# One more pair of feature tiles on the seven-product path of the second FFN, its operands made ready inside w_o

## The chip, the cores and the metric

The kernel runs on one core of a Trainium2 chip. The engines that matter here: TensorE (PE) multiplies matrices; VectorE (DVE), ScalarE (ACT) and GpSimd (POOL) do elementwise work; SyncE (SP) issues the DMAs that load weights. Each engine works through its own instructions in order and waits where an operand, or the memory for a result, isn't there yet. The metric is the device time of one execution in microseconds (us), the median of several runs.

## The reference, cut to what matters

One layer of a streaming encoder on 512 tokens of width 1024, all in float32: FFN 1, a mixer (recurrent branch and attention, merged, then `w_o`), FFN 2, each between two RMS norms. The change touches the end of the mixer and FFN 2:

```python
def swiglu(x, w1, w3, w2):
    return (jax.nn.silu(x @ w1) * (x @ w3)) @ w2

h = h + rms_norm(merged @ w_o[l], mix_post_g[l])
f = swiglu(rms_norm(h, ffn2_pre_g[l]), ffn2_w1[l], ffn2_w3[l], ffn2_w2[l])
h = h + 0.5 * rms_norm(f, ffn2_post_g[l])
```

`D_FF` is 2816, so w1 and w3 have 22 feature tiles of 128 columns each.

## The kernel before

**Split numbers.** TensorE multiplies in a rounded float32 format (fp32r). To keep float32 accuracy each operand is split into hi, a cast on ACT, and lo, the operand less hi, a subtract on DVE (`split2`, L191 and L192; the same two lines for plain weight tiles in `split_to`, L156 and L157). A product takes three matmuls: hi hi, lo hi, hi lo.

**Units and pair jobs.** A plain unit (`unit`, `mm_feat`, L201 to L203) makes one feature tile for all 512 tokens: 8 slices of k, three matmuls of 512 columns each, 24 in all. From some feature tile on, two tiles go together as pair jobs (class `Pairs`), one for w1 and one for w3: the product is seen as 2 x 2 blocks (two halves of k, two halves of the tokens, two feature tiles) and made by seven block products instead of eight (Strassen's scheme in Winograd's form). One block product (`mm_s`, L452 to L454) is 4 slices of k, three matmuls of 256 columns each, so a pair job has 84. The price is sums of blocks: S1 to S4 of each weight pair (L497 to L500, on POOL unless `eng` says otherwise), T1 to T4 of the activations (`sums`, L728 to L732), and all of them are split again. `Pairs.prep(m, i)` makes job m's weights ready in five steps: 0 the sums S12 and S34, 1 the split of the first raw tile, 2 of S12, 3 of S34, 4 of the half tile a22. While job n runs, `Pairs.run` issues steps 1 to 4 of job n + 1, step 0 of job n + 2 and the loads of job n + 3. `hooks` lets other work be issued inside a job. The order inside a job is a11, s1 (with T1), the last product of the job before (a22 with T4), s2 (with T2), a12, s4, s3 (with T3).

`NC1` = 6 and `NC2` = 4 say from which feature tile on FFN 1 and FFN 2 use pair jobs. In FFN 2 tiles 0 and 1 belong to the end of w_o's stage (below), tiles 2 and 3 are plain units (`swiglu_units`), tiles 4 to 21 are 18 pair jobs.

**w_o's stage** (`tok_gemm`). The first two of w_o's eight k slices are multiplied for all four token tiles first. Then, token tile by token tile, come the other six slices (L219 to L221); when a token tile t is whole, `norms` adds it to h and norms it for FFN 2: two Squares on ACT (L259), fg on DVE (L260, L261), some small steps, the new h (L264), Squares and products again (L275, L276), and the result hg (L282 on DVE for one half of the columns, L283 on ACT for the other). TensorE transposes hg (L292), `transpose_out` copies and splits it into uT (L301 ACT, L302 DVE), and `transpose_xf` copies it unsplit into xf (L309 ACT), from which the sums T are made. TensorE transposes tile t after the matmuls of tile t + 1. Instead of a fifth tile's matmuls come those of FFN 2's first four weight tiles (w1 and w3 of feature tiles 0 and 1, `first`) on the first 256 tokens: after the first of them the transposes of token tile 2, before the last those of tile 3. Then the same four weight tiles on the other 256 tokens, then `tok_gemm` ends.

**What sets the order.** The program's order is kept on each engine. `later(n, fn)` issues something n points further on; a point comes after every four k slices of a unit and after each block product. Weight tiles are loaded and split in the order of a list (`order`); splitting ahead stops at the first paired tile, whose raw tile `Pairs` takes instead.

**Slots.** All large tiles share 42 slots of SBUF (`NSLOT`), 4 KB per partition each. A tile takes a slot at its first write and gives it back after its last use. With none free, the instruction that writes first waits, and what is behind it on its engine.

**Ahead of the first pair job** of FFN 2, before: its steps 0 to 4, T1 to T4 and the splits of T1 to T3 are issued by `later` during the four plain units of tiles 2 and 3.

Of the kernel before, what the change touches and what calls it, by code (L numbers as in the profile page):

```python
# [13 lines left out]
ALU = mybir.AluOpType  # L14
# [37 lines left out]
def hybrid_layer(ctx: ExitStack, tc: tile.TileContext, a: dict, out: bass.AP):  # L52
# [91 lines left out]
    def dma_to(n):  # L144
        while st["dma"] < min(n, len(order)):
            dma_one(st["dma"])
            st["dma"] += 1
# [148 lines left out]
    def transpose_out(banks, t, xf=None):  # L296
        c = slice(t * P, (t + 1) * P)
        for half, ps in enumerate(banks):
            ks = slice(half * 4, half * 4 + 4)
            v = ps.rearrange("p (k c) -> p k c", k=4)  # L300
            act.activation(uT[:, 0, ks, c], v, AF.Copy)  # L301
            dve.tensor_tensor(out=uT[:, 1, ks, c], in0=v, in1=f32(uT[:, 0, ks, c]), op=ALU.subtract)  # L302
        if xf:
            transpose_xf(banks, t, xf)
# [4 lines left out]
            act.activation(xf[half, t // 2][:, :, (t % 2) * P : (t % 2 + 1) * P], v, AF.Copy)  # L309


    def tok_gemm(nm, xs, n, R, gpost_name, scale, gpre_name, first, x_to=None, xf=None, spill=False):

        F = n - R
        acc = {}
        w = {}

        def accs(t):  # L320
            if t not in acc:
                acc[t] = [bank("acc"), bank("acc")]
            return acc[t]

        pre = min(2, F)
        x_to = x_to or (lambda k: None)
        for k in range(pre):
            x_to(k + 1)
            w[k] = get(nm, k, ahead=pre - k + 1)
        if pre:  # L330
            for tt in ((0, 1), (2, 3)):
                for k in range(pre):
                    for t in tt:
                        mm_tok(accs(t), xs[k], t, w[k], k == 0, False)
                        if t % 2:
                            point()
        for k in range(pre, F):
            x_to(k + 2)
            w[k] = get(nm, k, ahead=2 + (R - 2) * (k + 1) // F)
            for t in range(NT):  # L340
                mm_tok(accs(t), xs[k], t, w[k], k == 0, False)
                if t % 2:
                    point()
        point(True)
        for k in range(F, n):
            x_to(k + 1)
            w[k] = get(nm, k, ahead=max(0, n - 1 - k), rawahead=2)
        gpost = bcast(gpost_name)
        gpre = bcast(gpre_name) if gpre_name else None
        us, trs = {}, {}  # L350
        split_to(st["get"] + len(first))
        dma_to(st["split"] + 2)
        for t in range(NT):
            for ns in ((0,), (1,)):
                for k in range(F, n):
                    mm_tok(accs(t), xs[k], t, w[k], k == 0, k == n - 1, ns)
            if not gpre_name:
                o = slot([P, D], name="o")

                def store(nn, c, t=t, o=o):  # L360
                    sp.dma_start(out=out[t * P : (t + 1) * P, c], in_=o[:, c])

                post_norm(acc[t], t, gpost, scale, o, store)
                continue
            if t == NT - 1:
                break
            if t >= 1:
                trs[t - 1] = transpose_mm(us[t - 1])
            if t == NT - 2:

                transpose_out(trs[t - 1], t - 1)
            us[t] = norms(acc[t], t, gpost, scale, gpre, spill)
            if t == NT - 2 and xf:
                transpose_xf(trs[t - 1], t - 1, xf)
            elif t == 1:
                transpose_out(trs[t - 1], t - 1, xf)
        if not gpre_name:
            return
        t = NT - 1
        ws, bs = [], []  # L380
        for i, key in enumerate(first):
            ws.append(get(*key, ahead=len(first) - 1 - i, rawahead=2))
            bs.append(bank("f"))
            if i == len(first) - 1:
                trs[t] = transpose_mm(us[t])
                transpose_out(trs[t], t)
                if xf:
                    transpose_xf(trs[t - 1], t - 1, xf)
                    transpose_xf(trs[t], t, xf)
            mm_feat(bs[i], ws[i], 0, 256)  # L390
            if i == 0:
                trs[t - 1] = transpose_mm(us[t - 1])
                us[t] = norms(acc[t], t, gpost, scale, gpre, spill)
                transpose_out(trs[t - 1], t - 1)
        get_ahead()
        for w_, b in zip(ws, bs):
            mm_feat(b, w_, 256, 512)
        return bs
# [58 lines left out]
    class Pairs:  # L457
# [13 lines left out]
        def prep(self, m, i, eng=None):  # L471
            if m >= len(self.jobs) or (m, i) in self.ready:
                return
            self.ready.add((m, i))
            k = self.k0 + 2 * m
            if i == 0:
                if k not in loaded or k + 1 not in loaded:
                    self.raws(m)
                s12, s34 = slot([P, 2 * QH], name="S12"), slot([P, 2 * QH], name="S34")
                self.w[m] = {"r": (raws.pop(k), raws.pop(k + 1)), "s": (s12, s34)}  # L480
            W = self.w[m]
            (ra, rb), (s12, s34) = W["r"], W["s"]
            a11, a12, a21, a22 = ra[:, :QH], ra[:, QH:], rb[:, :QH], rb[:, QH:]

            def both(src, w=2 * QH):
                hi = slot([P, w], F32R, name="whi")
                lo = slot([P, w], F32R, name="wlo")
                split2(hi, lo, src)
                return hi, lo

            def halves(p, a, b):
                W[a] = p[0][:, :QH], p[1][:, :QH]
                W[b] = p[0][:, QH:], p[1][:, QH:]

            if i == 0:
                e = eng or pool
                e.tensor_tensor(out=s12[:, :QH], in0=a21, in1=a22, op=ALU.add)  # L497
                e.tensor_tensor(out=s12[:, QH:], in0=s12[:, :QH], in1=a11, op=ALU.subtract)
                e.tensor_tensor(out=s34[:, QH:], in0=a12, in1=s12[:, QH:], op=ALU.subtract)
                e.tensor_tensor(out=s34[:, :QH], in0=a11, in1=a21, op=ALU.subtract)  # L500
            elif i == 1:
                halves(both(ra), "a11", "a12")
            elif i == 2:
                halves(both(s12), "s1", "s2")
            elif i == 3:
                halves(both(s34), "s3", "s4")
            elif i == 4:
                t = slot([P, 2, QH], F32R, name="w22")
                split2(t[:, 0, :], t[:, 1, :], a22)
                W["a22"] = t[:, 0, :], t[:, 1, :]  # L510
                del W["r"], W["s"]

        def run(self, tail, hooks={}):
# [208 lines left out]
    def pair_view(p):  # L722
        return lambda e, k: p[e][:, k, :]

    def sums(xf):

        t = [slot([P, 4, 256], name="T") for _ in range(4)]
        pool.tensor_tensor(out=t[2], in0=xf[1, 1], in1=xf[0, 1], op=ALU.subtract)  # L728
        dve.tensor_tensor(out=t[0], in0=xf[0, 1], in1=xf[0, 0], op=ALU.subtract)
        dve.tensor_tensor(out=t[1], in0=xf[1, 1], in1=t[0], op=ALU.subtract)  # L730
        dve.tensor_tensor(out=t[3], in0=xf[1, 0], in1=t[1], op=ALU.subtract)
        return t  # L732

# [20 lines left out]
    for k in range(KT):  # L754
        later(2 + k // 2, lambda k=k: norm_x(k))
    later(6, lambda: xts.clear())
    later(6, lambda: tn.extend(sums(xn)))
    later(7, lambda: X1.update(b11=to_slots(xn[0, 0])))
    later(9, lambda: X1.update(t1=to_slots(tn[0])))
    later(11, lambda: X1.update(t2=to_slots(tn[1])))  # L760
# [359 lines left out]
    del xh, xl, OH, OL, KS, QS, BT  # L1120
    h_load([h_scr[t] for t in range(NT)])
    xf = {(hh, th): slot([P, 4, 256], name="xf") for hh in range(2) for th in range(2)}
    bs = tok_gemm("wo", mg, KT, RO, "mix_post_g", 1.0, "ffn2_pre_g", [("w1b", 0), ("w3b", 0), ("w1b", 1), ("w3b", 1)], xf=xf)


    hid = Hidden()
    X2, tn = {"b11": uview(0, 0), "b21": uview(1, 0), "b22": uview(1, 1)}, []
    later(1, lambda: hid.f.append(silu_mul(bs[0], bs[1])))
    later(2, lambda: hid.f.append(silu_mul(bs[2], bs[3])))
    later(1, lambda: tn.extend(sums(xf)))  # L1130
    later(2, lambda: xf.clear())
    for i in range(3):
        later(2 + i, lambda i=i: X2.update({f"t{i + 1}": to_slots(tn[i])}))
    pairs_b = Pairs("w1b", "w3b", NC2, X2, hid)
    end = 2 * 2 * (NC2 - 2)
    for i, at_ in enumerate((end - 7, end - 4, end - 3, end - 2, end - 1)):
        later(at_, lambda i=i: pairs_b.prep(0, i))
    later(end, lambda: pairs_b.prep(1, 0))
    swiglu_units("w1b", "w3b", 2, NC2, hid)
    point(True)  # L1140
    X2["t4"] = to_uT(tn[3], 0, 1)
    tn.clear()
    pairs_b.run(w2_ahead)
    X2 = pairs_b = None
    tok_gemm("w2b", hid, FT, RF, "ffn2_post_g", 0.5, None, [], hid.to)

# [12 lines left out]
RO = 6  # L1159

NC1 = 6
NC2 = 4


# [52 lines left out]
```

## Time and profile before

| | us |
|---|---|
| median of 3 runs (1138.37 to 1138.80) | 1138.46 |
| the profiled execution | 1138.66 |
| its span, first to last instruction | 1136.9 |
| TensorE busy | 1128.2 (99%) |
| VectorE busy | 778.7 (68%) |
| ScalarE busy | 582.2 (51%) |
| GpSimd busy | 340.7 (30%) |
| mean granted TensorE clock | 0.998 of full speed |

The page's parts: busy time by engine; the span in slices; DMA queues; the chain of work that ended last, followed back from the end, with the share of each engine and line; the costliest groups of instructions. In a timeline a row is: start and duration in us, engine, line, operation, result <- operands, partitions x elements, count, and in brackets how long the engine was idle before it and who released it. Matmuls overlap in their recorded durations, so their pace is read from their starts.

### The profile page before, as it was taken

The page shows a single profiled execution, that of the slowest core. Times are in us where ns is not written, and L with a number is a line of the kernel's source. Part 1 is how long each engine was busy: PE and PEld are TensorE (multiplying, and loading weights), DVE is VectorE, ACT ScalarE, POOL GpSimd, SP SyncE. Part 2 cuts the span into 40 slices and gives each one's busy share as a digit, 9 for nine tenths or more (in the row PEclk, how much of TensorE's full clock was granted, in tenths as well). Part 3 has the DMA queues.
Part 4 walks back from the last instruction along what each step waited for, and adds up shares of the span by engine and source line. Part 5 has one row for each costly group of instructions (what it writes and reads, how often), then busy time and mean ns, then how long its engine had stood idle before and what let it go on. Part 6 is the DMA issues. An engine that isn't in the chain of part 4 may idle for free.

```text
span 1136.9 us, 17091 instructions
## 1 busy us (share of the span) xinstructions
PE 1128.2 (99%) x6691; PEld 1001.0 (88%) x6691; DVE 778.7 (68%) x1183; ACT 582.2 (51%) x1036; POOL 340.7 (30%) x257
## 2 busy tenths in 40 slices
PE   9999999999999999999999999999999999999997
PEld 7889999988889977888888888889899999998886
DVE  5997889885436745684778854667968678985313
ACT  7445555564325369944656652356445555574211
POOL 0148677500001000001555640000655567700000
PEclk9999999999999999999999999999999999999999
DMA  9943223264314311334122333532123332254101
GB/s 343 158 132 112 96 92 111 82 216 157 104 55 146 132 56 56 90 96 130 56 85 83 93 109 98 176 118 93 39 93 112 112 103 84 93 193 176 40 19 55
DMA packets 36800, 124.93 MB, mean 110 GB/s; under 512 B 4400, under 2 KB 5936, under 8 KB 36720
## 3 DMA queue, kind: packets, MB, share of 16 engines
q1 hardware_dynamic: 34128, 115.15, 30.3%
q0 software_dynamic: 2448, 8.43, 3.8%
q8 instruction: 52, 0.85, 0.3%
q10 hardware_dynamic: 144, 0.26, 0.1%
q14 instruction: 28, 0.23, 0.1%
HBM read 116.50 MB, written 7.33 MB: 109 GB/s over the span
## 4 chain that ended last, share of the span: by engine, by line
PE 97%; DVE 2%; ACT 0%; issue 0%; DVEq 0%
PE f L201 11%; PE f L202 11%; PE f L203 11%; PE c L454 10%; PE c L453 10%; PE c L452 10%; PE acc L220 8%; PE acc L221 8%; PE acc L219 8%; PE pt L1032 1%; PE s L996 1%; PE s L995 1%; PE tr L292 1%; PE r L832 1%; PE o L1048 1%; PE o L1049 1%
## 5 line engine op out<-in xcount | busy, mean ns | idle before, releaser
L201 PE MATMUL f<-uT,whi 128*128 128x512 f32 (+1 forms) x536 | 197.1, 368 | 0.0
L202 PE MATMUL f<-uT,wlo 128*128 128x512 f32 (+1 forms) x536 | 195.3, 364 | 0.3 <-DVE wlo L157 0.3
L203 PE MATMUL f<-uT,whi 128*128 128x512 f32 (+1 forms) x536 | 195.0, 364 | 0.0
L219 PE MATMUL acc<-whi,hT 128*128 128x512 f32 x352 | 137.1, 390 | 0.0
L220 PE MATMUL acc<-wlo,hT 128*128 128x512 f32 x352 | 137.0, 389 | 0.0
L221 PE MATMUL acc<-whi,hT 128*128 128x512 f32 x352 | 136.9, 389 | 0.0
L201 PEld LDWEIGHTS f<-uT,whi 128*128 128x128 f32 x536 | 101.1, 189 | 18.4 <-issue 2.9
L192 DVE TENSOR_TENSOR wlo<-S,whi 128x1024 fp32r<-128x1024 f32 x68 | 112.9, 1660 | 4.0 <-ACT whi L191 3.7
L453 PE MATMUL c<-Xh,wlo 128*128 128x256 f32 x408 | 115.5, 283 | 0.0
L454 PE MATMUL c<-Xl,whi 128*128 128x256 f32 x408 | 115.5, 283 | 0.0
L453 PE MATMUL c<-uT,wlo 128*128 128x256 f32 x408 | 115.5, 283 | 0.0
L454 PE MATMUL c<-uT,whi 128*128 128x256 f32 x408 | 115.5, 283 | 0.0
L452 PE MATMUL c<-Xh,whi 128*128 128x256 f32 x408 | 115.5, 283 | 0.0
L452 PE MATMUL c<-uT,whi 128*128 128x256 f32 x408 | 115.5, 283 | 0.0
L202 PEld LDWEIGHTS f<-uT,wlo 128*128 128x128 f32 x536 | 101.2, 189 | 16.1 <-DVE wlo L157 0.7
L203 PEld LDWEIGHTS f<-uT,whi 128*128 128x128 f32 x536 | 101.1, 189 | 16.1
L1016 POOL TENSOR_SCALAR P<-P,d 128x256 f32<-128x256 f32 (+1 forms) x64 | 63.8, 1011 | 55.5 <-DVE d L1014 33.2
L452 PEld LDWEIGHTS c<-Xh,whi 128*128 128x128 f32 x408 | 78.3, 192 | 0.0
L452 PEld LDWEIGHTS c<-uT,whi 128*128 128x128 f32 x408 | 78.3, 192 | 0.0
L453 PEld LDWEIGHTS c<-uT,wlo 128*128 128x128 f32 x408 | 78.3, 192 | 0.0
L453 PEld LDWEIGHTS c<-Xh,wlo 128*128 128x128 f32 x408 | 78.3, 192 | 0.0
L454 PEld LDWEIGHTS c<-Xl,whi 128*128 128x128 f32 x408 | 78.3, 192 | 0.0
(309 smaller groups left out, 2684.5 us busy)
## 6 DMA issues: line engine op xcount, KB each, us to landing
raw_w2a<-in_w2a_dram SPq DMA_DIRECT2D x22, 512.0 KB, 3.7
raw_w1b<-in_w1b_dram SPq DMA_DIRECT2D x22, 512.0 KB, 4.0
raw_w3b<-in_w3b_dram SPq DMA_DIRECT2D x22, 512.0 KB, 3.9
raw_w2b<-in_w2b_dram SPq DMA_DIRECT2D x22, 512.0 KB, 4.2
raw_w3a<-in_w3a_dram SPq DMA_DIRECT2D x21, 512.0 KB, 4.4
raw_w1a<-in_w1a_dram SPq DMA_DIRECT2D x20, 512.0 KB, 4.4
raw_wg<-in_wg_dram SPq DMA_DIRECT2D x16, 512.0 KB, 3.8
raw_xr<-in_xr_dram SPq DMA_DIRECT2D x8, 512.0 KB, 4.1
```

Source lines behind the costliest of these rows:

```text
L192: dve.tensor_tensor(out=lo, in0=src, in1=f32(hi), op=ALU.subtract)
L201: pe.matmul(ps[:, c0:c1], wh[:, s], h_, start=k == 0, stop=False)
L202: pe.matmul(ps[:, c0:c1], wl[:, s], h_, start=False, stop=False)
L203: pe.matmul(ps[:, c0:c1], wh[:, s], l_, start=False, stop=k == KT - 1)
L219: pe.matmul(acc[n], x[:, 0, c], wh[:, s], start=first, stop=False)
L220: pe.matmul(acc[n], x[:, 0, c], wl[:, s], start=False, stop=False)
L221: pe.matmul(acc[n], x[:, 1, c], wh[:, s], start=False, stop=last)
L292: pe.transpose(ps[:, k * P : (k + 1) * P], hg[:, kk * P : (kk + 1) * P], ident)
L452: pe.matmul(ps, wh[:, s], xh, start=first, stop=False, skip_group_check=True)
L453: pe.matmul(ps, wl[:, s], xh, start=False, stop=False, skip_group_check=True)
L454: pe.matmul(ps, wh[:, s], xl, start=False, stop=k == 3, skip_group_check=True)
L1016: pool.tensor_scalar(out=pt[:, x, b0:256], in0=pt[:, x, b0:256], scalar1=d[:, x : x + 1], scalar2=None, op0=ALU.mult)
```

## The change

`NC2` goes from 4 to 2: feature tiles 2 and 3 of FFN 2 become two pair jobs like the others, twenty instead of eighteen, and the four plain units go. The first pair job now comes right after `tok_gemm`. What was issued during the units is placed anew:

- `tok_gemm` takes `aside`, functions issued at given places: -1 ahead of the token loop, 0 to 2 behind the norm of that token tile, 3 behind the last transposes. Steps 0 (on POOL) and 1 of the first job go to -1, step 2 behind tile 0, step 3 behind tile 1, step 4 behind tile 2.
- `operands`, at 3: a tiny Silu, the sums T1 to T4, all on DVE now (T3 was on POOL), the splits of T1 and T2.
- After `tok_gemm`: the Silu product of feature tile 0, the split of T3, step 0 of the second job on DVE instead of POOL, its step 1, the Silu product of feature tile 1.
- The split of T4 is issued inside the first job, after its first product, instead of ahead of it.
- `sums` takes the engine of T3 as an argument. In FFN 1 it stays POOL; only the order of the line changes.

```diff
+        aside = [aside.get(t, lambda: None) for t in (0, 1, 2, 3, -1)]
...
         split_to(st["get"] + len(first))
         dma_to(st["split"] + 2)
+        aside[-1]()
         for t in range(NT):
...
             elif t == 1:
                 transpose_out(trs[t - 1], t - 1, xf)
+            aside[t]()
...
                     transpose_xf(trs[t], t, xf)
+                aside[t]()
             mm_feat(bs[i], ws[i], 0, 256)
...
+            if all((m, x) in self.ready for x in range(5)):
                 del W["r"], W["s"]
...
-    def sums(xf):
+    def sums(xf, eng):
         t = [slot([P, 4, 256], name="T") for _ in range(4)]
-        pool.tensor_tensor(out=t[2], in0=xf[1, 1], in1=xf[0, 1], op=ALU.subtract)
         dve.tensor_tensor(out=t[0], in0=xf[0, 1], in1=xf[0, 0], op=ALU.subtract)
         dve.tensor_tensor(out=t[1], in0=xf[1, 1], in1=t[0], op=ALU.subtract)
+        eng.tensor_tensor(out=t[2], in0=xf[1, 1], in1=xf[0, 1], op=ALU.subtract)
         dve.tensor_tensor(out=t[3], in0=xf[1, 0], in1=t[1], op=ALU.subtract)
...
-    later(6, lambda: tn.extend(sums(xn)))
+    later(6, lambda: tn.extend(sums(xn, pool)))
...
-    hid = Hidden()
-    X2, tn = {"b11": uview(0, 0), "b21": uview(1, 0), "b22": uview(1, 1)}, []
-    later(1, lambda: hid.f.append(silu_mul(bs[0], bs[1])))
-    later(2, lambda: hid.f.append(silu_mul(bs[2], bs[3])))
-    later(1, lambda: tn.extend(sums(xf)))
-    later(2, lambda: xf.clear())
-    for i in range(3):
-        later(2 + i, lambda i=i: X2.update({f"t{i + 1}": to_slots(tn[i])}))
+    hid, tn = Hidden(), []
+    X2 = {"b11": uview(0, 0), "b21": uview(1, 0), "b22": uview(1, 1)}
     pairs_b = Pairs("w1b", "w3b", NC2, X2, hid)
-    end = 2 * 2 * (NC2 - 2)
-    for i, at_ in enumerate((end - 7, end - 4, end - 3, end - 2, end - 1)):
-        later(at_, lambda i=i: pairs_b.prep(0, i))
-    later(end, lambda: pairs_b.prep(1, 0))
-    swiglu_units("w1b", "w3b", 2, NC2, hid)
-    point(True)
-    X2["t4"] = to_uT(tn[3], 0, 1)
-    tn.clear()
-    pairs_b.run(w2_ahead)
+    def operands():
+        act.activation(small(4, "tiny")[:, 0:1], vec[:, 0:1], AF.Silu)
+        tn.extend(sums(xf, dve))
+        X2["t1"] = to_slots(tn[0])
+        X2["t2"] = to_slots(tn[1])
+    bs = tok_gemm(
+        "wo", mg, KT, RO, "mix_post_g", 1.0, "ffn2_pre_g", [("w1b", 0), ("w3b", 0), ("w1b", 1), ("w3b", 1)], xf=xf,
+        aside={-1: lambda: [pairs_b.prep(0, i) for i in (0, 1)], 0: lambda: pairs_b.prep(0, 2), 1: lambda: pairs_b.prep(0, 3), 2: lambda: pairs_b.prep(0, 4), 3: operands})
+    xf.clear()
+    hid.f.append(silu_mul(bs[0], bs[1]))
+    X2["t3"] = to_slots(tn[2])
+    pairs_b.prep(1, 0, dve)
+    pairs_b.prep(1, 1)
+    hid.f.append(silu_mul(bs[2], bs[3]))
+    del bs
+    late = {(0, 1): [lambda: X2.update(t4=to_uT(tn[3], 0, 1)), tn.clear]}
+    pairs_b.run(w2_ahead, late)
...
-NC2 = 4
+NC2 = 2
```

More of the change, by code (lines that the diff above doesn't have):

```diff
@@ L309, in transpose_xf, with tok_gemm @@
             act.activation(xf[half, t // 2][:, :, (t % 2) * P : (t % 2 + 1) * P], v, AF.Copy)
-    def tok_gemm(nm, xs, n, R, gpost_name, scale, gpre_name, first, x_to=None, xf=None, spill=False):
+    def tok_gemm(nm, xs, n, R, gpost_name, scale, gpre_name, first, x_to=None, xf=None, spill=False, aside={}):
+        aside = [aside.get(t, lambda: None) for t in (0, 1, 2, 3, -1)]
         F = n - R
@@ L1122, in hybrid_layer @@
     xf = {(hh, th): slot([P, 4, 256], name="xf") for hh in range(2) for th in range(2)}
-    bs = tok_gemm("wo", mg, KT, RO, "mix_post_g", 1.0, "ffn2_pre_g", [("w1b", 0), ("w3b", 0), ("w1b", 1), ("w3b", 1)], xf=xf)
-    hid = Hidden()
-    X2, tn = {"b11": uview(0, 0), "b21": uview(1, 0), "b22": uview(1, 1)}, []
-    later(1, lambda: hid.f.append(silu_mul(bs[0], bs[1])))
-    later(2, lambda: hid.f.append(silu_mul(bs[2], bs[3])))
-    later(1, lambda: tn.extend(sums(xf)))
-    later(2, lambda: xf.clear())
-    for i in range(3):
-        later(2 + i, lambda i=i: X2.update({f"t{i + 1}": to_slots(tn[i])}))
-    pairs_b = Pairs("w1b", "w3b", NC2, X2, hid)
-    end = 2 * 2 * (NC2 - 2)
-    for i, at_ in enumerate((end - 7, end - 4, end - 3, end - 2, end - 1)):
-        later(at_, lambda i=i: pairs_b.prep(0, i))
-    later(end, lambda: pairs_b.prep(1, 0))
-    swiglu_units("w1b", "w3b", 2, NC2, hid)
-    point(True)
-    X2["t4"] = to_uT(tn[3], 0, 1)
-    tn.clear()
-    pairs_b.run(w2_ahead)
+    hid, tn = Hidden(), []
+    X2 = {"b11": uview(0, 0), "b21": uview(1, 0), "b22": uview(1, 1)}
+    pairs_b = Pairs("w1b", "w3b", NC2, X2, hid)
+    def operands():
[15 more added lines that the diff above has]
+    pairs_b.run(w2_ahead, late)
     X2 = pairs_b = None
```

## The prediction

> **What bounds the kernel now.** I read the page's first part and its chain, then TensorE's own timeline around the change, then ScalarE (ACT) and VectorE (DVE) over the same microseconds.
>
> ```profile
> PE 1128.2 (99%) x6691; PEld 1001.0 (88%) x6691; DVE 778.7 (68%) x1183; ACT 582.2 (51%) x1036; POOL 340.7 (30%) x257
> PE 97%; DVE 2%; ACT 0%; issue 0%; DVEq 0%
> 806.96:828.75 21.79, 21.79 (x98) 18.03 (x97) 16.60 (x12) 8.65 (x11) 10.04 (x7) 1.00 0.30 97
> 828.75:1010.18 181.43, 181.43 (x1513) 181.43 (x1512) 142.03 (x152) 99.61 (x174) 107.77 (x63) 1.00 0.32 105
> 806.96 0.40 PE L201 MATMUL f<-uT,whi 128*128 128x512 f32 x1
> 828.75 0.28 PE L452 MATMUL c<-uT,whi 128*128 128x256 f32 x1
> 1010.18 0.40 PE L219 MATMUL acc<-whi,hT 128*128 128x512 f32 x1
> ```
>
> TensorE is the whole path: 99% busy, 97% of the chain, clock 1.00 in both windows (columns: length, then busy time by engine, clock, DMA share, GB/s). So the change is worth what it takes off TensorE, less every microsecond in which it makes TensorE wait. The last three rows mark the stage: plain units of feature tiles 2 and 3 from 806.96 to 828.75, then 18 pair jobs until 1010.18.
>
> **What the change removes and adds on TensorE.** Out go four units (w1 and w3 of tiles 2 and 3): 21.79 us. In come two pair jobs: 181.43 / 18 = 10.08 us each, 20.16 us. Saved: 1.63 us, not an eighth of 21.79 (2.72), since 84 narrow matmuls take 10.08 / 84 = 0.120 us each where half of a wide one (21.79 / 96 = 0.227) is 0.113. [...] The rows say 1.63, and the sum goes by them.
>
> **What covers the preparation.** Before, the four units hid the first pair job's work: its S12/S34 sums on GpSimd, its casts and subtracts, the sums T of the activations. Without them the weights' splits move into w_o's token loop. Is there room?
>
> ```profile
> 763.24 0.72 ACT L283 ACTIVATE hg<-hg,r 128x512 f32<-128x512 f32 x1 [0.93 <-DVE r L243]
> 763.87 0.58 ACT L259 ACTIVATE junk<-acc 128x512 f32<-128x512 f32 x1
> 770.97 0.73 ACT L283 ACTIVATE hg<-hg,r 128x512 f32<-128x512 f32 x1 [0.87 <-DVE r L243]
> 771.60 1.06 ACT L301 ACTIVATE uT<-tr 128x512 fp32r<-128x512 f32 x2
> 772.94 1.19 ACT L309 ACTIVATE xf<-tr 128x512 f32<-128x512 f32 x2 [0.27 <-DVE uT L302]
> 774.03 1.08 ACT L301 ACTIVATE uT<-tr 128x512 fp32r<-128x512 f32 x2
> 774.99 0.61 ACT L259 ACTIVATE junk<-acc 128x512 f32<-128x512 f32 x1
> 776.04 0.23 ACT L259 ACTIVATION_READ_ACCUMULATOR junk<-acc 128x1 f32 x1
> 782.25 0.72 ACT L283 ACTIVATE hg<-hg,r 128x512 f32<-128x512 f32 x1 [0.87 <-DVE r L243]
> 783.84 0.60 ACT L259 ACTIVATE junk<-acc 128x512 f32<-128x512 f32 x1
> ```
> ```profile
> 758.93 0.75 DVE L264 SCALAR_TENSOR_TENSOR h<-fg,r,h 128x512 f32<-128x512 f32 x1
> 764.57 0.69 DVE L260 TENSOR_TENSOR fg<-acc,bc_mix_post_g 128x512 f32<-128x512 f32 x1 [0.91 <-ACT junk L259]
> 774.66 1.29 DVE L302 TENSOR_TENSOR uT<-tr,uT 128x512 fp32r<-128x512 f32 x2 [1.15 <-ACT uT L301]
> 775.86 0.68 DVE L260 TENSOR_TENSOR fg<-acc,bc_mix_post_g 128x512 f32<-128x512 f32 x1
> 784.56 0.69 DVE L260 TENSOR_TENSOR fg<-acc,bc_mix_post_g 128x512 f32<-128x512 f32 x1 [1.82 <-ACT junk L259]
> 791.03 0.48 DVE L282 TENSOR_SCALAR hg<-hg,r 128x512 f32<-128x512 f32 x1
> ```
> ```profile
> 772.89 1.03 PE L292 MATMUL tr<-ident,hg 128*128 128x128 f32 x8
> 784.81 1.04 PE L292 MATMUL tr<-ident,hg 128*128 128x128 f32 x8
> 791.31 0.28 PE L203 MATMUL f<-uT,whi 128*128 128x256 f32 x1
> 791.67 1.06 PE L292 MATMUL tr<-ident,hg 128*128 128x128 f32 x8
> ```
>
> No. From 763.87 each token tile's norm starts where the last one's work ends on ACT: hg (L283), uT and xf copies, the next Squares (L259). This one row of work ends with hg of token tile 3 at 791.03 + 0.48 = 791.51, and TensorE transposes that tile at 791.67, 0.24 us after its last matmul could have ended (791.31 + 0.12). The cover of this row is already used up: what is put into it for token tiles 1 to 3 is a wait of TensorE. Prices of what is put in:
>
> ```profile
> 744.49 1.22 DVE L157 TENSOR_TENSOR wlo<-raw_w1b,whi 128x1024 fp32r<-128x1024 f32 x1
> 745.62 1.22 DVE L157 TENSOR_TENSOR wlo<-raw_w3b,whi 128x1024 fp32r<-128x1024 f32 x1
> 748.88 1.06 ACT L156 ACTIVATE whi<-raw_w3b 128x1024 fp32r<-128x1024 f32 x1 [0.80 <-DMA raw_w3b<-in_w3b_dram]
> 749.98 1.23 DVE L157 TENSOR_TENSOR wlo<-raw_w3b,whi 128x1024 fp32r<-128x1024 f32 x1 [0.64 <-ACT whi L156]
> 814.08 0.62 ACT L191 ACTIVATE w<-raw_w1b 128x512 fp32r<-128x512 f32 x1
> 829.02 0.69 DVE L410 TENSOR_TENSOR sw<-f,sw 128x512 f32<-128x512 f32 x1 [5.43 <-PE f L203]
> 829.63 2.30 DVE L192 TENSOR_TENSOR uT<-T,uT 128x1024 fp32r<-128x1024 f32 x1
> 751.00:752.00 1.00, 1.00 (x6) 0.84 (x5) 0.20 (x1) 0.22 (x1) 0.00 (x0) 1.00 0.00 0
> ```
>
> A split is a cast of 1.05 on ACT and, 0.04 after its end (748.88 + 1.06 to 749.98), a subtract that holds DVE for 1.13 (744.49 to 745.62). ACT starts its next step 0.09 before the last one's recorded end (763.24 + 0.72 against 763.87), so a cast holds it for 0.96. A half-width split is a cast of 0.62 (ACT held for 0.53) and a subtract that holds DVE for about 0.61, as the half-width product at 829.02 does until 829.63.
>
> - **Ahead of token tile 0** (S12/S34 sums on POOL, split of the first raw tile): no cost. The raw loads are done by 751 (DMA share 0.00 in the window 751:752; two tiles are fetched there now as then, another one second). The split ends by 751 + 1.05 + 0.04 + 1.23 = 753.3, ahead of all that norm 0 does with its second half of columns. The POOL sums, four of 1.28 from 751 on (row 826.81 below), some slower beside the split, end near 757; the norm's first long step on DVE with two SBUF inputs starts at 758.93.
> - **After tile 0** (split of S12): the cast takes 763.87 to 764.92, DVE is free at 764.96 + 1.13 = 766.09 where fg began at 764.57: **1.52** late. The cast itself waits for nothing: POOL's S12 is there since 757. Behind it on ACT stand norm 1's Squares, behind the subtract on DVE its fg. Tile 1's hg is whole at 770.97 + 0.73 + 1.52 = 773.2 and TensorE comes for it at 772.89, for its second half of columns 0.4 later: no more than 0.1 of a wait, and that is part of the next ones.
> - **After tile 1** (split of S34, between the xf and uT copies): cast at 774.03 + 1.52 = 775.55 to 776.60, subtract 776.64 to 777.77, then the two uT subtracts (774.66 to 775.86, 1.20): fg could start at 778.97. Slots make it a little later. Counted from the code, 34 of 42 slots are held here before (6 merged tiles, 12 w_o weights, 8 first weights, 2 raw tiles, 2 gains, 4 h); six split tiles and two xf tiles come on top, one raw tile goes: 41, and S34 itself holds the last. So the Squares' scratch must wait for S34's slot (subtract ends 777.87) and fg for the scratch: 777.91 + 1.28 (774.99 to 776.27, two Squares and the reads) + 0.03 = 779.22, that is **3.36** after 775.86.
> - **After tile 2** (half-width split of a22, behind xf on ACT): the Squares of tile 3 at 783.84 + 3.36 + 0.53 = 787.73; on DVE the subtract starts at 787.20 + 0.62 + 0.04 = 787.86 and fg at 788.47: **3.9** after 784.56. So tile 3's transposes come at 791.67 + 3.9 = 795.6, and TensorE with them; about 1.4 of it is waited out already at tile 2's transposes (hg done at 782.25 + 0.72 + 3.36 = 786.3, its first half a little sooner; TensorE there at 784.81).
> - **First job's operands.** What is late next would be T1 and T2:
>
> ```profile
> 793.57 2.08 ACT L309 ACTIVATE xf<-tr 128x512 f32<-128x512 f32 x4
> 798.51 1.28 ACT L409 ACT_TABLE_LOAD   x1
> 799.15 2.31 DVE L157 TENSOR_TENSOR wlo<-raw_w3b,whi 128x1024 fp32r<-128x1024 f32 x1
> 800.46 2.16 POOL L498 TENSOR_TENSOR S<-S,raw_w1b 128x512 f32<-128x512 f32 x1
> 826.81 1.28 POOL L497 TENSOR_TENSOR S<-raw_w1b 128x512 f32<-128x512 f32 x1 [7.77 <-DMA raw_w1b<-in_w1b_dram]
> ```
>
> xf ends at 793.57 + 2.08 + 3.9 = 799.5. DVE then does four sums and two subtracts, 6 x 1.13 = 6.8, to 806.4; the Silu table load (1.28) is beside it on ACT, only moved. TensorE reaches the first job at 806.96 + 3.9 = 810.9 and needs T1 1.44 and T2 2.88 later (12 matmuls by 0.120 each). Margin 6 to 7 us, so no wait. Silu product, T3, the next job's sums on DVE (4 by 0.61) and its first split, and the second Silu product add 5.9 us, to 812.3, against 819.5 for the second job (six products of 1.44). T4's split inside the first job is needed after 822 and is done near 814. The loads of w3's two raw tiles, next in SP's queue, take slots that TensorE frees from 778.5 on (784.81 less 24 matmuls by 0.12, less five k slices of 3 x 0.227), and SP has nothing else to do there. None of it is on the path; if a load came late, the sums on DVE would hold up T4 and the second job's splits behind them (the rival below). Behind the jobs nothing else moves; one slot is freed.
>
> If GpSimd runs beside DVE the prices double: 2.31 where the same subtract takes 1.22, and 2.16 against 1.28 on POOL. [...] No row here has POOL beside a norm; my dates put its end ahead of it.
>
> **The sum.** +3.9 - 1.63 = +2.3 us. The profiled run had 1138.66 (span 1136.9), 0.2 above the median; on the median: 1138.46 + 2.3 = **1140.7**. Faster by 0.2% (2.28 us, about what a measurement tells) is out of reach of the matmuls' 1.63; the other border, 1140.74, runs through my forecast.
>
> Bounds of what the trace lacks: slots, nothing (-0.25) to a wait for tiles that TensorE frees one by one from 778.5, each 0.68 later (+2); POOL running into norm 0, 0 to +1; first job, 0 to +3.
>
> **The rivals.**
> - *DVE's gaps swallow the subtracts.* DVE idles 0.91, 1.15 and 1.82 us ahead of three quoted rows. If only the casts count: 0.96 + 0.96 + 0.53 = 2.45, net +0.8: 1139.2, not slower. Against it: each gap ends just when a cast on ACT would end, and the subtract waits for that cast. It decides if fg of tile 2 begins before 778.3.
> - *Everything hides.* Only the 1.63 and the idle 0.24 remain: 1136.6, within 0.2%. It needs slack ahead of 791.67, and there is none.
> - *Slots decide.* ACT or DVE waits in norm 2 for tiles held until TensorE's second pass over tile 3; each further slice 0.68: +1 to +2 on top, 1141.5 to 1142.7.
> - *The first pair starves.* With POOL beside, six DVE steps take 13.6 instead of 6.8 and T2 comes at 813.1 against 813.8; with a late raw tile ahead of them in DVE's order the job waits up to 3: 1141 to 1144.
>
> **How the numbers follow.** Forecast (net +1.9 to +2.6) 0.53; gaps swallow 0.16; all hides 0.04; slots 0.16; starving 0.11. The forecast's chance is halved by the border: 0.26 same, 0.27 slower. Same: 0.26 + 0.16 + 0.03 = 0.45. Slower: 0.27 + 0.16 + 0.11 = 0.54. Faster 0.01. The range takes in most of the gaps' case with a few tenths around it and all but the far end of starving, and leaves out the case where all hides: 1138.9 to 1143.3. Around the forecast alone it would be 1140.3 to 1141.1.
>
> **What would show it.** fg of the four norms 0, 1.5, 3.4 and 3.9 later; TensorE idle near 1.4 us ahead of tile 2's transposes and 2.7 ahead of tile 3's, none ahead of tile 1's; first job at 810.9 with no gap after it; twenty jobs of 10.08; last norm work unchanged in length. I am wrong if tile 3's transposes start before 794 or after 797, or if TensorE waits inside the first two jobs.

## The result, and the profile after

The changed kernel takes 1142.78 us (median of 5 runs, 1142.52 to 1142.93) beside 1138.76 of the kernel before (5 runs): a ratio of 1.0036, 95% interval 1.0025 to 1.0048. It is 4.0 us slower; I had said 2.3. Timed again among the later runs it took 1142.88 beside 1138.66, ratio 1.0037 (1.0025 to 1.0049).

The profiled execution (1142.78, span 1141.0 where the one before had 1136.9) loses 5.7 us in one stretch of 28 us (785.0 to 812.7) and wins 1.6 back in the pair jobs behind it. From the page's first part and TensorE's timeline of the changed kernel (start, duration, engine, line, operation; in brackets the idle time and its releaser):

```profile
PE 1128.4 (99%) x6763; PEld 1004.2 (88%) x6763; DVE 787.8 (69%) x1199; ACT 588.0 (52%) x1050; POOL 339.9 (30%) x260
```
```profile
785.02 0.28 PE L203 MATMUL f<-uT,whi 128*128 128x256 f32 x1
786.52 1.06 PE L292 MATMUL tr<-ident,hg 128*128 128x128 f32 x8 [1.23 <-DVE hg L282]
...
793.06 0.28 PE L203 MATMUL f<-uT,whi 128*128 128x256 f32 x1
795.90 1.06 PE L292 MATMUL tr<-ident,hg 128*128 128x128 f32 x8 [2.57 <-DVE hg L282]
...
797.05 0.41 PE L203 MATMUL f<-uT,whi 128*128 128x256 f32 x1
797.27 0.41 PE L201 MATMUL f<-uT,whi 128*128 128x256 f32 x1
...
800.46 0.28 PE L201 MATMUL f<-uT,whi 128*128 128x256 f32 x1
800.58 0.28 PE L202 MATMUL f<-uT,wlo 128*128 128x256 f32 x1
...
812.68 0.28 PE L457 MATMUL c<-uT,whi 128*128 128x256 f32 x1
...
1014.28 0.40 PE L219 MATMUL acc<-whi,hT 128*128 128x512 f32 x1
```

Two waits stand ahead of the transposes of token tiles 2 and 3: 785.02 + 0.12 to 786.52 is 1.4 us, 793.06 + 0.12 to 795.90 is 2.7. The second is the end of the norm chain: 795.90 instead of 791.67, so 4.23 later. Then comes what I had not foreseen: from 797.05 narrow matmuls start 0.21 to 0.22 us apart, and from 800.46 0.12 apart again. The windows of the changed kernel say what this is (length, busy time of PE, PEld, DVE, ACT, POOL, then the granted clock, DMA share, GB/s):

```profile
793.18:795.90 2.72, 0.16 (x2) 0.03 (x1) 2.09 (x7) 1.56 (x5) 0.00 (x0) 1.00 0.00 0
797.05:800.46 3.41, 3.41 (x19) 3.41 (x18) 2.98 (x5) 3.39 (x7) 0.00 (x0) 0.50 0.00 0
812.68:1014.28 201.60, 201.60 (x1682) 201.60 (x1681) 161.35 (x169) 110.40 (x193) 120.62 (x72) 1.00 0.32 106
```

For 3.41 us, from 797.0 on, TensorE had half its clock. The idle stretch had ended 1.1 us before; the transposes in between still ran at the full clock (0.99 from 795.90 to 797.05). The price of the half clock: from tile 3's transposes to the first pair job it now takes 812.68 - 795.90 = 16.78 us, where the same work, up to the first plain unit, took 806.96 - 791.67 = 15.29: 1.5 us. The twenty pair jobs take 201.60 / 20 = 10.08 each, as before, without a gap. So +4.23 (chain) + 1.49 (half clock) - 1.63 (matmuls) = +4.1, which is 1014.28 - 1010.18, the shift at the end of the jobs. Behind them nothing has changed.

DVE, ACT and POOL of the changed kernel, at the places of the prediction's steps:

```profile
752.64 0.68 DVE L260 TENSOR_TENSOR fg<-acc,bc_mix_post_g 128x512 f32<-128x512 f32 x1
758.92 0.75 DVE L264 SCALAR_TENSOR_TENSOR h<-fg,r,h 128x512 f32<-128x512 f32 x1
...
764.99 1.23 DVE L192 TENSOR_TENSOR wlo<-S,whi 128x1024 fp32r<-128x1024 f32 x1 [1.28 <-ACT whi L191]
766.13 0.68 DVE L260 TENSOR_TENSOR fg<-acc,bc_mix_post_g 128x512 f32<-128x512 f32 x1
...
776.86 1.23 DVE L192 TENSOR_TENSOR wlo<-S,whi 128x1024 fp32r<-128x1024 f32 x1 [1.67 <-issue]
779.42 0.69 DVE L260 TENSOR_TENSOR fg<-acc,bc_mix_post_g 128x512 f32<-128x512 f32 x1
...
788.19 0.69 DVE L192 TENSOR_TENSOR w<-raw_w1b,w 128x512 fp32r<-128x512 f32 x1 [1.81 <-ACT w L191]
788.80 0.68 DVE L260 TENSOR_TENSOR fg<-acc,bc_mix_post_g 128x512 f32<-128x512 f32 x1
...
804.17 2.35 DVE L192 TENSOR_TENSOR Xl<-T,Xh 128x1024 fp32r<-128x1024 f32 x2
```
```profile
778.12 0.60 ACT L259 ACTIVATE junk<-acc 128x512 f32<-128x512 f32 x1 [0.38 <-DVE wlo L192]
```
```profile
756.55 1.30 POOL L505 TENSOR_TENSOR S<-raw_w1b,raw_w1b 128x512 f32<-128x512 f32 x1
```

Each split (L192) stands ahead of the next norm's fg (L260), that of S34 also ahead of the two uT subtracts (1.28): the norms' fg come 0.1 (752.50 before), 1.56, 3.56 and 4.24 later than before. The Squares at 778.12 wait for a DVE subtract that they share no data with; by the prediction's count of slots they wait for the slot of S34. POOL's last sum ends at 757.85, ahead of the norm's step at 758.92. The two fg steps of that norm ran beside POOL's sums (752.64 and 756.70) and took 0.68 each, as before (0.69 and 0.68).

One note for what follows: the profiled execution of the run a22_late (1869 us) and two of fill_part (1239 and 4551 us) were disturbed, so of a22_late only the times of the other ten are used, and of fill_part the other ten with its profile.

### The profile page after: what moved, and what is told of

Read it like the earlier page. It is cut to its first block, busy times and chain, and to the rows that moved or that the text cites. A ratio compares the mean times of both kernels' runs of the same rounds, so it can differ in the third digit from the quotient of the medians.

```text
span 1141.0 us, 17275 instructions
## 1 busy us (share of the span) xinstructions
PE 1128.4 (99%) x6763; PEld 1004.2 (88%) x6763; DVE 787.8 (69%) x1199; ACT 588.0 (52%) x1050; POOL 339.9 (30%) x260
## 4 chain that ended last, share of the span: by engine, by line
PE 94%; DVE 4%; ACT 1%; issue 1%; DMA 0%; SPq 0%; DVEq 0%; ACTq 0%
PE c L459 11%; PE c L458 11%; PE c L457 11%; PE f L201 11%; PE f L202 10%; PE f L203 10%; PE acc L221 8%; PE acc L220 8%; PE acc L219 8%; PE pt L1038 1%; PE s L1002 1%; PE s L1001 1%; PE r L838 1%; PE o L1054 1%; PE o L1055 1%
## 5 line engine op out<-in xcount | busy, mean ns | idle before, releaser
L201 PE MATMUL f<-uT,whi 128*128 128x512 f32 (+1 forms) x504 | 185.3, 368 | 0.0
L202 PE MATMUL f<-uT,wlo 128*128 128x512 f32 (+1 forms) x504 | 183.5, 364 | 0.3 <-DVE wlo L157 0.3
L203 PE MATMUL f<-uT,whi 128*128 128x512 f32 (+1 forms) x504 | 183.3, 364 | 0.0
L459 PE MATMUL c<-Xl,whi 128*128 128x256 f32 x432 | 122.3, 283 | 0.0
L457 PE MATMUL c<-uT,whi 128*128 128x256 f32 x432 | 122.3, 283 | 0.0
L458 PE MATMUL c<-uT,wlo 128*128 128x256 f32 x432 | 122.3, 283 | 0.0
L459 PE MATMUL c<-uT,whi 128*128 128x256 f32 x432 | 122.3, 283 | 0.0
L458 PE MATMUL c<-Xh,wlo 128*128 128x256 f32 x432 | 122.3, 283 | 0.0
L457 PE MATMUL c<-Xh,whi 128*128 128x256 f32 x432 | 122.2, 283 | 0.0
L192 DVE TENSOR_TENSOR wlo<-S,whi 128x1024 fp32r<-128x1024 f32 x72 | 117.1, 1626 | 7.3 <-ACT whi L191 5.2
L201 PEld LDWEIGHTS f<-uT,whi 128*128 128x128 f32 x504 | 95.9, 190 | 17.2 <-issue 2.9
L202 PEld LDWEIGHTS f<-uT,wlo 128*128 128x128 f32 x504 | 95.9, 190 | 14.8 <-DVE wlo L157 0.7
L203 PEld LDWEIGHTS f<-uT,whi 128*128 128x128 f32 x504 | 95.8, 190 | 14.8
L457 PEld LDWEIGHTS c<-uT,whi 128*128 128x128 f32 x432 | 82.9, 192 | 0.0
L459 PEld LDWEIGHTS c<-uT,whi 128*128 128x128 f32 x432 | 82.9, 192 | 0.0
```

The lines of the kernel that those rows point to most:

```text
L192: dve.tensor_tensor(out=lo, in0=src, in1=f32(hi), op=ALU.subtract)
L201: pe.matmul(ps[:, c0:c1], wh[:, s], h_, start=k == 0, stop=False)
L202: pe.matmul(ps[:, c0:c1], wl[:, s], h_, start=False, stop=False)
L203: pe.matmul(ps[:, c0:c1], wh[:, s], l_, start=False, stop=k == KT - 1)
L457: pe.matmul(ps, wh[:, s], xh, start=first, stop=False, skip_group_check=True)
L458: pe.matmul(ps, wl[:, s], xh, start=False, stop=False, skip_group_check=True)
```

## Experiments

Three questions: does the wait come from the three splits in the norm chain (theory A) or from the pair jobs, their operands or the slots (rival B); does the half clock come from the idle stretch (A) or from something else at that place (rival C); do the sums belong on DVE (D)? Medians stand against the kernel before on the same chip (1138.6 or 1138.7, 17 to 27 runs each).

**late_steps: the three splits out of the norms.**

```diff
-        aside={-1: lambda: [pairs_b.prep(0, i) for i in (0, 1)], 0: lambda: pairs_b.prep(0, 2), 1: lambda: pairs_b.prep(0, 3), 2: lambda: pairs_b.prep(0, 4), 3: operands})
+        aside={-1: lambda: [pairs_b.prep(0, i) for i in (0, 1)], 3: lambda: [operands()] + [pairs_b.prep(0, i) for i in (2, 3, 4)]})
```

> The changed kernel with the splits of S12, S34 and a22 (steps 2 to 4 of the first job) taken out of the norms and issued behind the splits of T1 and T2. Theory A: the 4.1 us are +4.2 of waiting behind those three splits in the norms, +1.5 of half clock that follows the longest wait, -1.6 of matmuls. Then here no wait ahead of tile 2's transposes, at most the old 0.24 ahead of tile 3's, clock 1.00 throughout, first job at about 807.0, twenty jobs of 10.08, and 1138.8 - 1.6 = 1137.1 (1136.8 to 1137.6). Rival B, the three splits matter little and the first pair job or the slots cost the time: the norm waits shrink but TensorE waits at the first job's s1 or s2 instead (the splits are later now), 1139 or more.

Measured: 1137.49 (1136.89 to 1137.64), ratio 0.9989 (0.9980 to 0.9998). The change is now a gain. Its TensorE timeline, and DVE's at the one wait that is left:

```profile
791.48 0.28 PE L203 MATMUL f<-uT,whi 128*128 128x256 f32 x1
791.91 1.06 PE L292 MATMUL tr<-ident,hg 128*128 128x128 f32 x8
...
817.28 0.28 PE L457 MATMUL c<-Xh,whi 128*128 128x256 f32 x1
817.66 0.39 PE L458 MATMUL c<-Xh,wlo 128*128 128x256 f32 x1
```
```profile
813.65 1.72 DVE L192 TENSOR_TENSOR uT<-T,uT 128x1024 fp32r<-128x1024 f32 x1
815.29 2.31 DVE L192 TENSOR_TENSOR wlo<-S,whi 128x1024 fp32r<-128x1024 f32 x1
```

Tile 3's transposes wait 0.31 (0.24 in the kernel before), there is no other wait in the norms and no half clock: from these transposes to the second job's s1 it is 817.28 - 791.91 = 25.37, where the changed kernel needs 822.76 - 795.90 = 26.86, 1.49 more. So the three splits make the waits and all that follows from them; 5.3 us hang on their place. Of rival B 0.36 us is left: at 817.28 the second job's s1 starts before lo of its S12 is whole (815.29 + 2.31 = 817.60). T4's subtract stands ahead of it on DVE.

**before_with_splits: the splits alone, without the pair jobs.** Three needless splits are put into the kernel before, behind the same norms.

```diff
+            if t < extra:
+                wd = D if t < 2 else 512
+                dh, dl = slot([P, D], F32R, name="dhi"), slot([P, D], F32R, name="dlo")
+                split2(dh[:, :wd], dl[:, :wd], gpost[:, :wd])
```

> The kernel before, with its plain units of tiles 2 and 3 and nothing of the pair jobs moved, plus three needless splits (two of 1024 columns behind the norms of token tiles 0 and 1, one of 512 behind that of tile 2) into slots that nobody reads. Theory A: the norm chain is late by 1.5, 3.1 and 3.7 (no slot shortage here), TensorE waits about 1.1 and 2.6, and if the clock falls after the long wait another 1.5 is lost: 1138.8 + 3.7 + 1.5 = 1143.9; without the fall 1142.4. Rival B (the splits themselves cost little and the pair jobs or their operands do): under 1140.

Measured: 1143.95; four executions from 1143.58 to 1144.04, one at 1142.05. Ratio 1.0042 (1.0028 to 1.0056). From its timeline and its windows:

```profile
795.45 1.94 PE L292 MATMUL tr<-ident,hg 128*128 128x128 f32 x8 [2.57 <-DVE hg L282]
```
```profile
795.45:798.47 3.02, 3.02 (x14) 3.02 (x15) 2.30 (x4) 2.70 (x7) 0.00 (x0) 0.50 0.26 104
```

The kernel before has the same wait, the same half clock and a loss of 5.3 us once the splits stand in its norms. Pair jobs and slots aren't needed for it. The clock falls at about 795.2 here, 0.2 us before the wait ends: the 2.72 us ahead of 795.45 have 0.96 in the mean. The execution at 1142.05 fits the expectation's other case, a wait without the half clock (1142.4).

**fill_wait and fill_part: TensorE kept busy while it waits.** Needless matmuls (12, then 5) go ahead of tile 3's transposes, into a bank that is overwritten afterwards.

```diff
             if i == len(first) - 1:
+                for _ in range(FILL if xf else 0):
+                    pe.matmul(bs[i], ws[0][0][:, :P], ws[0][0][:, 512:], start=True, stop=True)
                 trs[t] = transpose_mm(us[t])
```

> The changed kernel with 12 needless matmuls of 512 columns (12 x 0.227 = 2.7 us of TensorE) ahead of tile 3's transposes, written to a bank that is overwritten afterwards; nothing else moves. Theory A, the half clock comes from TensorE standing idle for 2.7 us: the transposes stay at about 795.9, the clock stays at 1.00 after them, and the kernel gets 1.5 us faster by more work: 1141.3 (1141.1 to 1141.6). Rival C, the half clock comes from something else at that place: it stays at 0.50 for 3.4 us, 1142.8 or later. If the clock falls all the same but elsewhere, the wait of 1.4 us ahead of tile 2's transposes is enough for it.

> The changed kernel with 5 needless matmuls of 512 columns (1.1 us) ahead of tile 3's transposes instead of 12, so that TensorE still stands idle for about 1.6 us. Theory A with a limit on idle time (1.7 us of idle never brought the half clock in the run s12_only, 2.1 in two of ten, 2.7 in nearly all): clock 1.00, 1141.3 as with the wait filled whole. If the wait must be filled whole: 1142.8, half clock for 3.4 us.

Measured: 1141.29 (1141.01 to 1141.58) with 12, ratio 1.0023 (1.0014 to 1.0033); 1141.09 (1140.85 to 1141.78, ten executions) with 5, ratio 1.0022 (1.0013 to 1.0032), beside 1142.88 of the changed kernel on the same chip. Timeline and window of fill_wait, then of fill_part:

```profile
792.93 2.91 PE L390 MATMUL f<-whi 128*128 128x512 f32 x12
795.69 1.03 PE L292 MATMUL tr<-ident,hg 128*128 128x128 f32 x8
```
```profile
796.80:800.30 3.50, 3.50 (x32) 3.50 (x31) 3.06 (x5) 3.48 (x7) 0.00 (x0) 1.00 0.00 0
```
```profile
793.09 1.33 PE L390 MATMUL f<-whi 128*128 128x512 f32 x5
795.72 1.09 PE L292 MATMUL tr<-ident,hg 128*128 128x128 f32 x8 [1.31 <-DVE hg L282]
```
```profile
795.70:800.00 4.30, 4.28 (x36) 4.28 (x37) 3.15 (x5) 4.28 (x10) 0.00 (x0) 1.00 0.00 0
```

The transposes start within 0.2 us of where they did (795.7 for 795.9), the clock stayed at 1.00 and the kernel got 1.5 to 1.8 us faster by more work. The idle stretch is the cause of the half clock; rival C falls. It did not have to be filled whole: with 1.5 us of idle time behind five matmuls the clock stayed at 1.00 too.

> The changed kernel itself, beside the run fill_part on one chip: 1142.8 (1142.5 to 1143.0), half clock in all or nearly all executions. [...]

The repetition: 1142.72 to 1143.00 in five executions, none near the 1141.1 to 1141.3 of the filled wait. Its profile has the same wait:

```profile
795.85 1.37 PE L292 MATMUL tr<-ident,hg 128*128 128x128 f32 x8 [2.57 <-DVE hg L282]
```

The clock fell again: from 796 to 800 it is 0.57 in the mean, which is 3.4 us at 0.50, and from 799.96 on narrow matmuls start 0.12 apart again. So it fell at about 796.5, 0.6 us behind the wait's end where it was 1.1 in the first profile. By the times a stretch of 2.7 us brought the half clock in all ten executions of the changed kernel (mean granted clock 0.997 in each).

**a22_late and s12_only: one split less, two splits less in the norms.**

```diff
# a22_late
-        ... 1: lambda: pairs_b.prep(0, 3), 2: lambda: pairs_b.prep(0, 4), 3: operands})
+        ... 1: lambda: pairs_b.prep(0, 3), 3: lambda: [operands(), pairs_b.prep(0, 4)]})
# s12_only
+        ... 0: lambda: pairs_b.prep(0, 2), 3: lambda: [operands()] + [pairs_b.prep(0, i) for i in (3, 4)]})
```

> The changed kernel with only the half-width split of a22 moved from behind the norm of token tile 2 to behind the splits of T1 and T2. Theory A: tile 3's transposes come 0.6 sooner, the wait ahead of them is 2.1 instead of 2.7. If the clock still falls: 1142.2. If 2.1 us of idle time are too few for it: 1140.7. Rival B: no change, 1142.8.

> The changed kernel with only the split of S12 left behind the norm of token tile 0; those of S34 and a22 are issued behind T2's split. Theory A (every split in the norm chain is a delay of its DVE length, and the chain ends in TensorE's wait): tile 3's transposes 1.5 later than in the kernel before, at 793.2, a wait of about 1.8 ahead of them and none ahead of tile 2's (slack 2.0), clock 1.00 or nearly always: 1137.5 + 1.5 = 1139.0 (1138.8 to 1139.2). Rival (one split fits into the gaps of DVE and ACT, and only the later two hurt): 1137.5.

Measured: a22_late 1140.62, ratio 1.0019 (1.0010 to 1.0029); eight executions from 1140.39 to 1140.67, two at 1142.05 and 1142.24. s12_only 1138.92 (1138.58 to 1139.51), ratio 1.0003 (0.9994 to 1.0012). The transposes of s12_only:

```profile
793.49 0.74 PE L292 MATMUL tr<-ident,hg 128*128 128x128 f32 x5 [1.54 <-DVE hg L282]
```

With the changed kernel and late_steps this is a row of doses: no split in the norms 1137.5, one 1138.9 (+1.4), two 1140.6 (+3.1), all three without the half clock 1141.1 to 1141.3 (+3.6 to +3.8), with it 1142.8. No split fits into a gap of the chain, not even the first. The two executions of a22_late that are 1.5 to 1.7 above the others have the size of the half clock; that it is one wasn't seen in a trace.

**long_wait: the idle stretch made longer**, by a fourth split, a needless one, behind the norm of tile 2.

```diff
+            if t == NT - 2 and xf:
+                dh, dl = slot([P, D], F32R, name="dhi"), slot([P, D], F32R, name="dlo")
+                split2(dh, dl, gpost)
```

> The changed kernel with one more needless split of 1024 columns behind the norm of token tile 2, which makes the wait ahead of tile 3's transposes longer by 1.1: 3.8 instead of 2.7. Theory A: tile 3's transposes at 797.0. If the half clock is one window of 3.4 us set off by an idle stretch: again 3.4 us at 0.50 and 1142.8 + 1.1 = 1143.9. If its length grows with the idle time: over 1144.4. If the idle time is not what sets it off, no more than 1143.9 and the clock falls at the same microsecond as before.

Measured: 1144.27 to 1144.32 in four executions, and 1145.69 in the profiled one; ratio 1.0051 (1.0039 to 1.0064). Its windows:

```profile
796.10:797.55 1.45, 0.00 (x1) 0.04 (x1) 1.16 (x5) 0.64 (x2) 0.00 (x0) 0.52 0.00 0
797.55:802.90 5.35, 5.35 (x25) 5.35 (x26) 3.80 (x5) 5.01 (x10) 0.00 (x0) 0.50 0.00 0
```

The wait is 4.2 us, 1.5 longer (I had said 1.1: two casts follow each other on ACT and the second subtract waits for its own), and four executions are 1.4 to 1.5 later than the changed kernel: by these times the wait alone, with the same loss by the clock. In the profiled one the clock was down from about 796.1, while TensorE still waited, to 802.9: 6.8 us, twice 3.4. So here one wait cost 3.4 us of half clock, by the times, or 6.8. The start of the half clock isn't tied to the wait's end: in the four profiles that show one it lies 1.1 and 0.6 us behind it (changed kernel, changed_again) and 0.2 and 1.4 ahead of it (before_with_splits, long_wait).

**sums_on_pool: the sums back on GpSimd**, in the kernel of late_steps.

```diff
-        tn.extend(sums(xf, dve))
+        tn.extend(sums(xf, pool))
...
-    pairs_b.prep(1, 0, dve)
+    pairs_b.prep(1, 0)
```

> The kernel of the run late_steps with the changed engine undone: T3 and the four sums of the second job on GpSimd, as before the change, in place of DVE. Theory D (GpSimd beside DVE doubles the two-input steps of both, so the sums belong on DVE here): DVE's six steps to T2 and the first job's splits take twice as long while GpSimd runs, the S12 split ends near 808.5 where TensorE needs it at 808.9, and the first job waits 0 to 1.5: 1137.5 to 1139. Rival (DVE has fewer steps then, 0.6 x 4 + 1.1 less, and that outweighs the doubling): 1137.1 to 1137.5, the wait of 0.36 at the second job gone.

Measured: 1139.80, ratio 1.0010 (1.0002 to 1.0019), 2.3 over late_steps. DVE, POOL and TensorE of this run:

```profile
801.92 4.55 DVE L192 TENSOR_TENSOR Xl<-T,Xh 128x1024 fp32r<-128x1024 f32 x2
```
```profile
798.63 2.28 POOL L502 TENSOR_TENSOR S<-raw_w3b 128x512 f32<-128x512 f32 x1
```
```profile
836.54 0.28 PE L457 MATMUL c<-uT,whi 128*128 128x256 f32 x1
837.68 0.39 PE L458 MATMUL c<-uT,wlo 128*128 128x256 f32 x1 [0.86 <-DVE wlo L192]
```

Two later subtracts of DVE in this run, and the first of them in late_steps:

```profile
825.33 2.31 DVE L192 TENSOR_TENSOR wlo<-S,whi 128x1024 fp32r<-128x1024 f32 x1
837.55 2.30 DVE L192 TENSOR_TENSOR wlo<-S,whi 128x1024 fp32r<-128x1024 f32 x1
```
```profile
825.37 1.21 DVE L192 TENSOR_TENSOR wlo<-S,whi 128x1024 fp32r<-128x1024 f32 x1
```

The two splits of T1 and T2 take 4.55 beside POOL where the changed kernel needs 2.35 for the same rows, and POOL's steps take 2.28. TensorE waits at the first job's s1 (0.36), the second's (0.47), and most of it later, in the fourth job (1.0 and 0.7). That later loss isn't the first one carried along: with five sums fewer, DVE starts the split of the second job's S12 only 0.2 behind late_steps (815.48 and 815.29). It falls behind again. GpSimd's sums for the third job begin 3.6 us later than in late_steps (812.42 and 808.86) because their raw tile lands later, and from there GpSimd runs beside more of DVE's subtracts: from 812 to 842 it is busy for 27.9 us, where late_steps has 22.9. The subtract at 825.33 takes 2.31, where late_steps has 1.21 with GpSimd idle; that at 834.38 takes 1.78 and that at 837.55, whose result the fourth job's s1 waits for, 2.30, where the same shapes take 0.68 (809.77) and 1.21 (810.97) in this run with GpSimd idle. Why the raw tile lands later stays open. Theory D's doubling is there in these subtracts (4.55 for 2.35, 2.31 for 1.21) and in POOL's sums (2.28 where 1.30 is quoted from the changed kernel), but not in every two-input step of DVE: L415 took 0.68 at 813.24, beside POOL, as at 810.37 without it. The time is above the 1139 that I had given it at most, and the place of its price was further on. Part of the change is thus right: T3 and the second job's sums, moved together here, belong on DVE.

**t4_after_s12: late_steps with its last wait removed.** T4's split goes behind the split of the second job's S12.

```diff
                 self.prep(n + 1, 2)
+                at(4)
...
-    late = {(0, 1): [lambda: X2.update(t4=to_uT(tn[3], 0, 1)), tn.clear]}
+    late = {(0, 4): [lambda: X2.update(t4=to_uT(tn[3], 0, 1)), tn.clear]}
```

> The kernel of the run late_steps with T4's split inside the first job moved from behind its first product to behind the split of the second job's S12, which in that run came 0.3 us late for the second job. Theory A: that wait of 0.36 goes and nothing takes its place: 1137.1. Rival: T4 is then late for the product that needs it (a22 with T4, 1.44 us after s1) and the wait only moves: 1137.5 or up to 1138.5.

Measured: 1137.09 (1136.72 to 1137.36), ratio 0.9986 (0.9977 to 0.9994): the lowest median of all, 1.5 below the kernel before. The subtract of S12 now comes first on DVE, and s1 of the second job runs through:

```profile
813.30 1.72 DVE L192 TENSOR_TENSOR wlo<-S,whi 128x1024 fp32r<-128x1024 f32 x1
814.94 2.31 DVE L192 TENSOR_TENSOR uT<-T,uT 128x1024 fp32r<-128x1024 f32 x1
```
```profile
816.93 0.28 PE L457 MATMUL c<-Xh,whi 128*128 128x256 f32 x1
817.05 0.28 PE L458 MATMUL c<-Xh,wlo 128*128 128x256 f32 x1
```

That is nearly all of the 1.63 that the matmuls save.

## Why the prediction was right or wrong

The direction and the place were right, and 1142.78 lies inside the range; the size, +2.3 for +4.0, was not.

- *Matmuls saved, 1.63:* right. Twenty jobs at 10.08 without a gap.
- *Ahead of token tile 0, no cost:* right. fg came 0.1 later, at 752.64, the second half's step at 758.92 as before (758.93), POOL done at 757.85.
- *After tile 0, fg 1.52 late:* 1.56. *After tile 1, 3.36 with the slots:* 3.56; the slot shortage that was counted from the code is there, at 778.12. *After tile 2, 3.9:* 4.24. The chain was mis-sized by 0.3, in small pieces.
- *TensorE waits of 1.4 and 2.7:* measured 1.4 and 2.7. Ahead of tile 1's transposes it was 0.24 (772.67 + 0.23 to 773.14), where I had 0.1 at most.
- *First job's operands, no wait:* right. T2's subtract ends at 804.17 + 2.35 = 806.5 (I had 806.4), the first job runs through.
- *The sum, +3.9 - 1.63:* this step failed. It lacks a term: the half clock behind the wait, 1.5 us. With it the first job came at 812.68, not at 810.9. I had read the clock as a constant 1.00 of this core and priced the wait by its length alone. fill_wait takes the wait's idle time away without its length, and the 1.5 us go. That the range held the result is luck: around the forecast alone I had 1140.3 to 1141.1, and the rest of the upper part came from rivals whose mechanisms did not happen: no wait on TensorE's second pass decided the slots, and the first pair did not starve.
- *DVE's gaps swallow the subtracts:* no. Each gap moved behind the cast that ends it, as argued; s12_only shows that even one split is paid in full.

The chances I gave to "within 0.2%" rested on the sum standing on the border; with the missing term it is 0.36% slower, the side that I had given 0.54.

The traces have the clock at 0.50 for 3.41 us in the changed kernel and for 6.8 in long_wait. By the times 2.7 us of idle time brought it in all ten executions of the changed kernel and in four of the five of before_with_splits, 2.1 us (a22_late, worked out from its times) in two of ten, 1.7 and 1.5 us (s12_only, fill_part) in none. The fall lies at another distance from the wait's end in each of the four profiles that show one; in the 3.4 us ahead of each, TensorE had stood idle for 2.3 to 2.8 us. No run moves the wait and keeps its length, so what sets the place of the fall, and why waits of 2.1 and 2.7 us brought it in some executions only, stays open.

## What to carry to other kernels

Before work is moved, find the chain of small steps that ends last in its new place, not the engine's busy share: DVE was 69% busy, and each split behind a norm still cost its length (1.4 us for the first, 1.7 for the second, 0.5 to 0.7 for the one of half width), since the norm chain had no gap of its own. The same splits 17 to 37 us later, behind the last transposes, cost no more than the 0.36 us that t4_after_s12 removes, and left the gain. And a wait of TensorE can have a second price, the half clock near its end: here 2.7 us of wait had it (0.50 for 3.4 us) in 14 of 15 executions, 2.1 in two of ten, by their times. If the wait can't be removed, a few needless matmuls in it can save more than they cost: 1.5 to 1.8 us here (fill_wait, fill_part).

## What the runs showed of the hardware that was not expected

- An idle stretch of TensorE of 2.7 us brought 3.4 us at half clock (0.50), which cost 1.5 us; they began between 0.2 us before the stretch's end and 1.1 behind it. 4.2 us of idle time brought 3.4 in four executions, by their times, and 6.8 in one; 1.5 and 1.7 us (fill_part, s12_only) none. With a little work in the stretch (five matmuls, 1.1 us, fill_part) the clock stayed at 1.00.
- GpSimd's price for DVE need not fall where the work was moved: with five sums back on GpSimd most of the lost time appears 30 us later, in the fourth pair job, where GpSimd's later sums run beside other subtracts of DVE (2.3 us for 1.2).
